# A fixed-order pipeline for the w_up stage of a diffusion block, with the w_down operands made in small steps

## The chip, the cores and the metric

The kernel runs on one core of one Trainium2 chip. The metric is the device time of one launch in microseconds, a median over several launches. One profiled execution gives the trace. The engines are named as in the profile: PE (matmuls), PEld (the weight loads of PE), DVE, ACT, POOL, and SP, which here only issues DMAs.

## The reference

One layer of a transformer-like block over 1024 tokens of width 1024, in float32. Two token mixers and their projections come first. What the change touches is the feed-forward part behind them:

```python
def swiglu(h, w_up, w_down):
    a, b = jnp.split(h @ w_up, 2, axis=-1)      # w_up: 1024 x 5632
    return (jax.nn.silu(a) * b) @ w_down        # w_down: 2816 x 1024
...
h2 = modulate(rmsnorm(x, g_ffn[l]), mod[:, 3, None], mod[:, 4, None])
x = x + mod[:, 5, None] * swiglu(h2, w_up[l], w_down[l])
return rmsnorm(x, g_final)
```

`mod` is one small matrix product of the conditioning vector, `silu(c) @ w_mod + b_mod`, in six parts of 1024.

## The kernel before, in words

**Arithmetic.** A float32 matrix product is made of three matmuls in a reduced format: each operand is split into a high part (a cast on ACT, L92) and a low part (value minus high part, on DVE, L93), and high x high, high x low and low x high add up in PSUM (`mm3`, L121 to L123). One matmul is 128x128 by 512 columns. A large product is split in 2x2 blocks and done with seven block products in place of eight (Strassen's method in Winograd's form). The operand forms are called B11, T2, T3, T1, B21, T4 and B22.

**The w_up stage** has 22 modules (`NFF`, m = 0 to 21), each 128 columns of a and 128 of b. A module loads two column blocks of w_up (`raw`, four buffers), makes four sums of them on POOL (`st`, L181, L182, L185, L195), splits seven weights (`op`, seven buffers) and runs seven products of 12 matmuls each. For m = 0 to 3 the products B11 and B21 are run earlier (`early`), so that 146 products are left. DVE adds each finished PSUM bank to the others (L184 to L200), ACT applies silu (L1017, L1020), DVE and POOL multiply (L1018, L1021), and ACT's queue stores the result to DRAM (`Gd`). The moving operands G are 28 tiles of 4 KB per partition which stay for the whole stage; the pool `slots` has 31 such places (`NS`).

**The operands of w_down.** The same stage also prepares w_down for the next one: 11 pairs of row blocks (`DPAIRS`), made between the modules m = 5 to 20 (`MADE_AT`). `down_operands` loads a pair, multiplies it by the gate row m5 on POOL (L1001, L1002), makes four differences on DVE (L1005 to L1009), splits seven forms into slots (`od`, ACT L92 and DVE L93) and stores each to DRAM by SP's queue (`Od`, L1012). The w_down stage loads them again (`form`, L1058) and casts them on ACT (L1060).

**The gate row m5** is made inside the stage: `mod_sum(5)` at m = 2 (eight 512 KB loads and eight DVE operations, L647 to L651), `mod_rows(5)` at m = 4 (L659 to L663).

**Order.** The kernel is written module by module. A planner puts the instructions of each engine's queue in an order by its own costs; each engine then runs its queue strictly in order, and an instruction that waits holds up all behind it. Only where the source says `manual_schedule` is the order of the text kept on each engine.

Of the kernel before, what the change touches and what calls it, by code (L numbers as in the profile page):

```python
# [8 lines left out]
F32 = mybir.dt.float32  # L9
F32R = mybir.dt.float32r  # L10
U8 = mybir.dt.uint8
AF = mybir.ActivationFunctionType
# [16 lines left out]
EPS = 1e-6  # L29
COL = dict(ff=0, fb=512, i=1024, q=1536, og=2048, u=2560, v=3072, ga=3584, gb=4608)  # L30
C_C, C_X, C_GM, C_GF, C_LB, C_GN, C_BM, NROW = 0, 8, 16, 24, 32, 48, 49, 97
NS = 31
RES = {1: (0, 4), 2: (1, 5), 3: (2, 6), 4: (3, 7)}
EARLY = ((), (0, 1), (2,), (3,))
H0, H1 = slice(0, HALF), slice(HALF, T)
# [3 lines left out]
def blk(i):  # L39
    return slice(i * P, (i + 1) * P)  # L40
# [3 lines left out]
def block_kernel(ctx: ExitStack, tc: tile.TileContext,  # L44
# [20 lines left out]
    def slot(name, shape=(P, T), dtype=F32):  # L65
        return slots.tile(list(shape), dtype, name=name, tag="s", bufs=NS)

    def op_slot(name):
        return slot(name, (P, 2, HALF), F32R)
# [4 lines left out]
    def ev_(name="ev"):  # L74
        return wp.tile([P, HALF], F32, name=name, tag="ev", bufs=8)

    def gl_(name="gl"):
        return wp.tile([P, HALF], F32, name=name, tag="gl", bufs=6)
# [10 lines left out]
    def split_into(o, v, hi_eng=act, lo_eng=dve):  # L89
        n = v.shape[-1]  # L90
        h, l = o[:, 0, :n], o[:, 1, :n]
        (act.copy if hi_eng is act else hi_eng.tensor_copy)(h, v)  # L92
        t_last[0] = lo_eng.tensor_tensor(l, v, h.bitcast(F32), op=ALU.subtract)  # L93
        return o
# [143 lines left out]
    def dtile(name, shape=(P, T)):  # L238
        return dram.tile(list(shape), F32, name=name)
# [3 lines left out]
    Id = [dtile(f"Id{t}", (P, HALF)) for t in range(TT)]  # L243
    Vd = [dtile(f"Vd{t}", (P, HALF)) for t in range(TT)]
    m2d = dtile("m2d")
    PBd = [dtile(f"PBd{m}") for m in range(KT)]
    X1d = [dtile(f"X1d{t}") for t in range(TT)]
    Gd = [dtile(f"Gd{m}", (P, 2, T)) for m in range(NFF // 2)]
# [393 lines left out]
    def mod_sum(j):  # L642

        a = slot("moda")
        for k in range(KT):
            raw = raw_()
            load(out=raw, in_=w_mod[blk(k), j * D:(j + 1) * D])  # L647
            if k == 0:
                dve.tensor_scalar(a, raw, sc[:, k, 0:1], None, op0=ALU.mult)
            else:  # L650
                dve.scalar_tensor_tensor(a, raw, sc[:, k, 0:1], a, op0=ALU.mult, op1=ALU.add)  # L651
        return a

    def mod_cols(j, a):
        part_sums(a, modc[:, j, :])
        dve.tensor_tensor(modc[:, j, :], modc[:, j, :], cols[:, C_BM + j * 8:C_BM + j * 8 + 8], op=ALU.add)

    def mod_rows(j, a, dst):
        load(out=dst, in_=b_mod[:, j * D:(j + 1) * D].broadcast_to([P, D]))  # L659
        for s in HS:  # L660
            ps = psx()
            pe.matmul(ps, ones, a[:, s], start=True, stop=True)
            dve.tensor_tensor(dst[:, s], ps, dst[:, s], op=ALU.add)  # L663

    rmask = const.tile([P, HALF], F32, name="rmask")
    dve.memset(rmask, 1.0)
    dve.memset(rmask.rearrange("p (c t) -> p c t", t=CH)[:, :, 0:1], 0.0)
    EA = const.tile([P, 8, 16], F32, name="EA")
# [46 lines left out]
    for n, (ka, fa, kb, fb) in enumerate(PAIRS):  # L715
        p_ = early[n] if n < len(early) else in_pair(n).head()
        if n == len(PAIRS) - 1:
            sg4 = slot("sg4", (P, 2, HALF))
            wsr, wsT = sg4[:, 0, :], sg4[:, 1, :]
            bsb = slot("bsb")[:, :HALF]  # L720
            load(out=wsr.rearrange("p (g s) -> p g s", s=P), in_=w_s[0].rearrange("g t s -> t g s"))
            load(out=bsb, in_=b_s.rearrange("a g t -> a (g t)").broadcast_to([P, HALF]))
        X, c12, c21, c22 = p_.rest(turn_ws if n == len(PAIRS) - 1 else None)
        if n == 0:
            with tc.issue_after(t_done.ins):
                for t in range(4):
                    vnorm(4 + t, vlate[t], dve)
        if ka[0] == "q":
            q = slot("q")
            act.copy(q[:, H0], X)  # L730
            pool.tensor_copy(q[:, H1], c12)
            for s, z in ((H0, c21), (H1, c22)):
                sg = gl_("sg")
                sig = after(lambda: act.activation(sg, z, AF.Sigmoid))
                pool.tensor_tensor(z, z, sg, op=ALU.mult)
                store(out=pd[kb][:, s], in_=z)
            table_use[0] = sig
            continue
        if ka[0] == "ff":
            e = ev_()  # L740
            zs = (e, c12, c21, c22)
            for z, src in zip(zs, (X, c12, c21, c22)):
                sig = after(lambda: act.activation(z, src, AF.Sigmoid))
            table_use[0] = sig
            gates(ka[1], zs, q)
        else:
            e = ev_()
            act.activation(e, X, fa)
            todo = ((ka, AF.Copy, H0, e), (ka, fa, H1, c12), (kb, fb, H0, c21), (kb, fb, H1, c22))
        for key, fn, s, z in (todo if ka[0] != "ff" else ()):  # L750
            if fn != AF.Copy:
                last_act = act.activation(z, z, fn)
            store(out=pd[key][:, s], in_=z)
        if n in (11, 13):
            ma = mod_sum({11: 3, 13: 4}[n])
        if n in (12, 14):
            mod_cols({12: 3, 14: 4}[n], ma)
        if n == 15:
            store(out=m2d, in_=mod_sum(2))
        if n == 7:  # L760
            act.activation(EA, EA, AF.Exp)
            E = EA.rearrange("p j (c i) -> p j c i", i=2)
            XA, GA, HA = (const.tile([P, 8, 8, 2], F32, name=nm) for nm in ("XA", "GA", "HA"))
            AP = const.tile([P, 8, 8], F32, name="AP")
            dve.memset(XA, 1.0)
            for dr in range(2):
                d_ = slice(4 * dr, 4 * dr + 4)
                a, b = (0, 1) if dr == 0 else (1, 0)
                Ea, Eb = E[:, d_, :, a], E[:, d_, :, b]
                X_ = XA[:, d_, :, 0]  # L770
                dve.tensor_tensor(X_, Ea, Eb, op=ALU.mult)
                dve.tensor_tensor(AP[:, d_, :], X_, X_, op=ALU.mult)
                dve.tensor_copy(GA[:, d_, :, a], Ea)
                dve.tensor_tensor(GA[:, d_, :, b], X_, Ea, op=ALU.mult)
                dve.tensor_copy(HA[:, d_, :, b], Eb)
                dve.tensor_tensor(HA[:, d_, :, a], X_, Eb, op=ALU.mult)
    dve.scalar_tensor_tensor(A2, modc[:, 4, :], 1.0, cols[:, C_GF:C_GF + 8], op0=ALU.add, op1=ALU.mult)


    V = [slot("V", (P, 2, HALF)) for _ in range(4)]  # L780
# [163 lines left out]
    def up_pair(m):  # L944
        return Strassen(lambda: load_cols(w_up, m * P, KT), lambda: load_cols(w_up, DFF + m * P, KT), G, 4)
# [41 lines left out]
                combine(F0[k][0], zs[0], F0[k][1], zs[1], k, G)  # L987

    SEG = [([0], [1])] + [([4 * i + 2, 4 * i + 3], [4 * i + 4, 4 * i + 5]) for i in range(5)]
    DPAIRS = [(ka, kb) for a, b in SEG for ka, kb in zip(a, b)]
    MADE_AT = {5 + 16 * i // 11: i for i in range(len(DPAIRS))}

    def down_operands(i):
        ka, kb = DPAIRS[i]
        ra, rb = (wp.tile([P, T], F32, name="rawd", tag="rawd", bufs=2) for _ in range(2))
        load(out=ra, in_=w_down[blk(ka), :])
        load(out=rb, in_=w_down[blk(kb), :])  # L1000
        pool.tensor_tensor(ra, ra, m5, op=ALU.mult)  # L1001
        pool.tensor_tensor(rb, rb, m5, op=ALU.mult)  # L1002
        x11, x12, x21, x22 = ra[:, H0], ra[:, H1], rb[:, H0], rb[:, H1]
        t1, t3, t4 = (gl_("t") for _ in range(3))
        dve.tensor_tensor(t1, x12, x11, op=ALU.subtract)  # L1005
        dve.tensor_tensor(t3, x22, x12, op=ALU.subtract)  # L1006
        t2 = x12
        dve.tensor_tensor(t2, x22, t1, op=ALU.subtract)
        dve.tensor_tensor(t4, x21, t2, op=ALU.subtract)  # L1009
        for nm, v in (("B11", x11), ("T1", t1), ("T3", t3), ("T2", t2), ("B22", x22), ("B21", x21), ("T4", t4)):  # L1010
            o = split_into(op_slot("od"), v)
            load(out=Od[nm, i], in_=o.bitcast(F32))  # L1012

    for m in range(NFF):
        X, c12, c21, c22 = (early[m] if m < len(early) else up_pair(m).head()).rest()
        e = ev_()
        act.activation(e, X, AF.Silu)  # L1017
        dve.tensor_tensor(e, e, c21, op=ALU.mult)  # L1018
        store(out=Gd[m // 2][:, m % 2, H0], in_=e)
        act.activation(c12, c12, AF.Silu)  # L1020
        pool.tensor_tensor(c12, c12, c22, op=ALU.mult)  # L1021
        store(out=Gd[m // 2][:, m % 2, H1], in_=c12)
        if m == 2:
            ma = mod_sum(5)
        if m == 4:
            m5 = slot("m5")
            mod_rows(5, ma, m5)
        if m in MADE_AT:
            down_operands(MADE_AT[m])


    X1 = [slot("X1") for _ in range(TT)]
# [147 lines left out]
                    for i in range(2):  # L1180
                        step(i, *st_)

    gs, O = [load_g(0, 0)], form(0)
    for s in range(len(SEG)):
        segment(s, O, gs)
        for t in RES.get(s, ()):
# [34 lines left out]
```

## Time and profile before

| what | value |
|---|---|
| median of 3 launches | 1564.56 us (1562.89 to 1566.66) |
| the profiled execution, its own time | 1563.21 us |
| its span, first to last instruction | 1561.5 us |
| PE busy | 1467.7 us, 94% of the span |
| DVE busy | 1111.4 us, 71% |
| ACT busy | 725.4 us, 46% |
| POOL busy | 610.5 us, 39% |

The span is 1.7 us shorter than the time of the same execution. PE's matmuls overlap one another: each takes some 0.39 us, and one starts every 0.23 us, so that a busy share says little and starts per microsecond say more.

### The profile page before, as it was taken

The numbers are of one execution on the slowest core, as the hardware profiler recorded it, in microseconds if no ns is written. First come the engines' busy times: TensorE is split into PE (matmuls) and PEld (weight loads), VectorE is DVE, ScalarE is ACT, GpSimd is POOL, SyncE is SP. The second block draws the span as 40 slices with busy tenths as digits, with TensorE's granted clock in tenths as the row PEclk, the third lists the DMA queues.
The fourth block names the chain that finished last, engine by engine and source line by source line (L and its number), as shares of the span: only waits on it lengthen the run. The fifth ranks groups of instructions, "written<-read, shape, count | busy, mean of one in ns | idle before, by whom it ended". The sixth has DMA issues, their size and how long they took to land. (4 is left out here: it accounts for less than half of the span.)

```text
span 1561.5 us, 19377 instructions
## 1 busy us (share of the span) xinstructions
PE 1467.7 (94%) x6754; PEld 1199.6 (77%) x6754; DVE 1111.4 (71%) x1530; ACT 725.4 (46%) x1214; POOL 610.5 (39%) x402
## 2 busy tenths in 40 slices
PE   6998999999999999999999899988878899999997
PEld 6887787777787787987788577766766788778886
DVE  2456676888767757775546987988889744577787
ACT  4355656766433332243255533334343334677645
POOL 0033143433233213344415545555464531444356
PEclk9799999999999999999999999999999999999999
DMA  9334532333677578624644163767677824599832
GB/s 308 97 121 135 149 109 68 121 122 115 209 232 228 187 256 297 225 73 133 218 148 173 58 195 115 251 237 274 240 264 257 282 82 150 187 346 357 300 115 108
DMA packets 208660, 294.41 MB, mean 189 GB/s; under 512 B 11601, under 2 KB 132018, under 8 KB 208562
## 3 DMA queue, kind: packets, MB, share of 16 engines
q1 hardware_dynamic: 183650, 245.45, 48.0%
q10 hardware_dynamic: 24912, 47.72, 8.2%
q8 instruction: 53, 0.87, 0.2%
q14 instruction: 45, 0.37, 0.1%
HBM read 202.95 MB, written 90.18 MB: 188 GB/s over the span
## 5 line engine op out<-in xcount | busy, mean ns | idle before, releaser
L93 DVE TENSOR_TENSOR op<-raw,op 128x512 fp32r<-128x512 f32 x208 | 187.4, 905 | 119.1 <-ACT op L92 118.9
L92 ACT CAST op<-raw 128x512 fp32r<-128x512 f32 x216 | 131.8, 620 | 178.4 <-PE acc L123 123.9
L121 PE MATMUL acc<-T,op 128*128 128x512 f32 x408 | 162.8, 400 | 20.9 <-DVE u L188 17.0
L121 PE MATMUL aux<-T,op 128*128 128x512 f32 x408 | 161.4, 396 | 14.2 <-DVE u L188 12.1
L122 PE MATMUL acc<-T,op 128*128 128x512 f32 x408 | 162.1, 397 | 4.8 <-DVE T L93 4.8
L93 DVE TENSOR_TENSOR op<-st,op 128x512 fp32r<-128x512 f32 x160 | 153.4, 960 | 11.8 <-ACT op L92 10.1
L123 PE MATMUL acc<-T,op 128*128 128x512 f32 x408 | 161.0, 395 | 0.0
L123 PE MATMUL aux<-T,op 128*128 128x512 f32 x408 | 160.5, 393 | 0.3 <-DVE op L93 0.3
L122 PE MATMUL aux<-T,op 128*128 128x512 f32 x408 | 160.1, 392 | 0.0
L92 ACT CAST op<-st 128x512 fp32r<-128x512 f32 x160 | 97.7, 618 | 119.3 <-PE aux L123 43.1
L181 POOL TENSOR_TENSOR st<-raw 128x512 f32<-128x512 f32 x40 | 65.4, 1635 | 193.5 <-DVE op L93 104.6
L121 PE MATMUL aux<-B,op 128*128 128x512 f32 x306 | 120.4, 393 | 8.9 <-DVE u L190 8.9
L121 PE MATMUL acc<-B,op 128*128 128x512 f32 x306 | 121.8, 398 | 7.4 <-DVE u L190 6.2
L195 POOL TENSOR_TENSOR st<-raw,st 128x512 f32<-128x512 f32 x40 | 59.9, 1498 | 155.9 <-DVE op L93 136.2
L122 PE MATMUL acc<-B,op 128*128 128x512 f32 x306 | 120.6, 394 | 0.0
L123 PE MATMUL acc<-B,op 128*128 128x512 f32 x306 | 120.6, 395 | 0.0
L123 PE MATMUL aux<-B,op 128*128 128x512 f32 x306 | 119.3, 390 | 0.4 <-DVE op L1136 0.4
L122 PE MATMUL aux<-B,op 128*128 128x512 f32 x306 | 119.3, 390 | 0.0
L121 PEld LDWEIGHTS acc<-T,op 128*128 128x128 f32 x408 | 77.8, 191 | 43.3 <-DVE u L188 21.2
L121 PEld LDWEIGHTS aux<-T,op 128*128 128x128 f32 x408 | 77.3, 189 | 35.0 <-DVE u L188 16.4
L122 PEld LDWEIGHTS acc<-T,op 128*128 128x128 f32 x408 | 78.1, 191 | 22.3 <-DVE T L93 6.7
L123 PEld LDWEIGHTS acc<-T,op 128*128 128x128 f32 x408 | 77.9, 191 | 16.3
(357 smaller groups left out, 3503.2 us busy)
## 6 DMA issues: line engine op xcount, KB each, us to landing
raw<-in_w_in_dram SPq DMA_DIRECT2D x60, 512.0 KB, 5.2
raw<-in_w_up_dram SPq DMA_DIRECT2D x46, 512.0 KB, 4.4
OdT<-od SPq DMA_DIRECT2D x44, 512.0 KB, 3.7
so<-OdT SPq DMA_DIRECT2D x44, 512.0 KB, 5.8
OdB<-od SPq DMA_DIRECT2D x33, 512.0 KB, 3.7
so<-OdB SPq DMA_DIRECT2D x33, 512.0 KB, 5.4
raw<-in_w_mod_dram SPq DMA_DIRECT2D x32, 512.0 KB, 4.1
rawd<-in_w_down_dram SPq DMA_DIRECT2D x22, 512.0 KB, 5.6
```

The source lines that it names most:

```text
L92: (act.copy if hi_eng is act else hi_eng.tensor_copy)(h, v)
L93: t_last[0] = lo_eng.tensor_tensor(l, v, h.bitcast(F32), op=ALU.subtract)
L121: pe.matmul(ps, lh, rh, start=first, stop=False, skip_group_check=cont)
L122: pe.matmul(ps, lh, rl, start=False, stop=False, skip_group_check=cont)
L123: pe.matmul(ps, ll, rh, start=False, stop=last, skip_group_check=cont)
L181: pool.tensor_tensor(s1, a21, a22, op=ALU.add)
L195: pool.tensor_tensor(s4, a12, s2, op=ALU.subtract)
```

## The change

The w_up stage is rewritten as one loop over all 146 products inside `manual_schedule`. At the step of product g, each engine's queue gets, in this order: the POOL sums of product g+5, the split of product g+4, the matmuls of g, the silu, gating and stores of earlier ones, the addition of the finished bank of g, and one or two of 13 small steps per pair of the w_down operands. These steps start at product 15 (m = 3) and are spread evenly to the end. The pair that the w_down stage uses first is made last and its seven forms stay in their slots (`made.kept`), so that it is neither stored nor loaded. Half of the multiplication by m5 moves from POOL to DVE. The gate row is made in the input projection (n = 15 and 16), kept in DRAM and loaded back; the sums for mod 3, 4 and 2 move to n = 9, 11 and 13. `NS` becomes 32; `rmask` takes a slot in place of a tile of its own.

```diff
-NS = 31
+NS = 32
-    rmask = const.tile([P, HALF], F32, name="rmask")
+    rmask = slot("rmask")[:, :HALF]
-        if n in (11, 13):
-            ma = mod_sum({11: 3, 13: 4}[n])
-        if n in (12, 14):
-            mod_cols({12: 3, 14: 4}[n], ma)
-        if n == 15:
+        if n in (9, 11, 15):
+            ma = mod_sum({9: 3, 11: 4, 15: 5}[n])
+        if n in (10, 12):
+            mod_cols({10: 3, 12: 4}[n], ma)
+        if n == 13:
             store(out=m2d, in_=mod_sum(2))
+        if n == 16:
+            m5r = slot("m5")
+            mod_rows(5, ma, m5r)
+            store(out=m5d, in_=m5r)
...
+    class DownOperands:
...
+        def hi(self, i, nm, v):
+            o = self.o[i, nm] = op_slot("od"), v
+            act.copy(o[0][:, 0, :], v)
+
+        def lo(self, i, nm):
+            o, v = self.o.pop((i, nm))
+            dve.tensor_tensor(o[:, 1, :], v, o[:, 0, :].bitcast(F32), op=ALU.subtract)
+            if i == self.pairs[-1]:
+                self.kept[nm] = [o]
+            else:
+                self.put.append((self.at, lambda: load(out=Od[nm, i], in_=o.bitcast(F32))))
+
+        def step(self, share, m5):
+            while self.at < min(self.n, share * self.n):
+                while self.put and self.put[0][0] < self.at:
+                    self.put.pop(0)[1]()
+                self.one(*self.steps[self.at], m5)
+                self.at += 1
...
+        def one(self, i, j, m5):
...
+            if j < 2:
+                for eng, z in ((dve, ra), (pool, rb)):
+                    eng.tensor_tensor(z[:, HS[j]], z[:, HS[j]], m5[:, HS[j]], op=ALU.mult)
...
+            elif j == 3:
+                t["T3"] = self.tile_("t")
+                dve.tensor_tensor(t["T3"], x22, x12, op=ALU.subtract)
+                self.hi(i, "B11", x11)
...
+            elif j == 5:
+                self.lo(i, "B11")
+                self.hi(i, "T2", x12)
...
+            elif j == 7:
+                self.lo(i, "T2")
+                if nxt is not None:
+                    self.fetch(nxt, 0)
+                self.hi(i, "B22", x22)
+            elif j == 8:
+                self.lo(i, "B22")
+                self.hi(i, "B21", x21)
+            elif j == 9:
+                self.lo(i, "B21")
+                if nxt is not None:
+                    self.fetch(nxt, 1)
+                self.hi(i, "T1", t["T1"])
+            elif j < 12:
+                nm, then = (("T1", "T3"), ("T3", "T4"))[j - 10]
+                self.lo(i, nm)
+                self.hi(i, then, t[then])
+            else:
+                self.lo(i, "T4")
...
+    LEAD = 4
+    NEW = ("B11", "T2", "T3", "T1", "B21", "T4", "B22")
+    prods = [(m, nm) for m in range(NFF) for nm in (NEW if m >= len(early) else ("T2", "T3", "T1", "T4", "B22"))]
...
+    made = DownOperands(list(range(1, len(DPAIRS))) + [0], gl_)
+    first_made = prods.index((3, "T2"))
+    with tc.manual_schedule():
+        up_loads(0)
+        up_loads(1)
+        m5 = last_gate()
+        for g in range(-LEAD - 1, N + 3):
+            if 0 <= g + LEAD + 1 < N:
+                up_sums(g + LEAD + 1)
+            if 0 <= g + LEAD < N:
+                up_split(g + LEAD)
+                m = prods[g + LEAD][0]
+                if ends[m] == g + LEAD and m + 2 < NFF:
+                    up_loads(m + 2)
+            if 0 <= g < N:
+                up_product(g)
+            for fn in todo_at.pop(g, ()):
+                fn()
+            if 0 <= g < N:
+                up_evac(g)
+            if g >= first_made:
+                made.step((g + 1 - first_made) / (N + 2 - first_made), m5)
+        made.step(1, m5)
...
-    gs, O = [load_g(0, 0)], form(0)
+    gs, O = [load_g(0, 0)], made.kept
```

## Rows read from the trace of the kernel before

**Rows 1.** The page: span and busy time of each engine

```profile
span 1561.5 us, 19377 instructions
PE 1467.7 (94%) x6754; PEld 1199.6 (77%) x6754; DVE 1111.4 (71%) x1530; ACT 725.4 (46%) x1214; POOL 610.5 (39%) x402
```

**Rows 2.** Busy us (instructions) by stretch: PE, PEld, DVE, ACT, POOL; clock, DMA share, GB/s

```profile
404.00:578.00 174.00, 170.28 (x774) 140.21 (x773) 114.34 (x144) 64.54 (x109) 42.91 (x31) 1.00 0.70 219
896.00:1250.00 354.00, 314.42 (x1305) 250.75 (x1306) 300.72 (x344) 133.67 (x235) 186.47 (x105) 0.97 0.68 233
980.00:1236.00 256.00, 220.37 (x905) 174.38 (x903) 221.71 (x252) 101.53 (x181) 136.72 (x74) 0.96 0.74 260
1250.00:1337.00 87.00, 87.00 (x386) 72.03 (x385) 37.20 (x55) 30.02 (x47) 22.67 (x19) 1.00 0.38 121
```

**Rows 3.** PE's matmuls with a T operand, 865 to 896 us: busy (instructions)

```profile
865.00:896.00 31.00, 18.32 (x62) 0.94 0.22 68
```

**Rows 4.** Who waited for whom, 896 to 1338 us: total us, times, longest us

```profile
PE acc L121 <- DVE u L188: 15.6, 5, 3.6
PE aux L121 <- DVE u L188: 10.6, 6, 3.7
PE acc L121 <- DVE u L190: 6.2, 3, 2.9
PE aux L121 <- DVE u L190: 4.7, 3, 2.2
...
ACT od L92 <- DMA OdT<-od: 68.6, 34, 3.7
ACT od L92 <- DMA OdB<-od: 39.3, 16, 4.6
...
DVE op L93 <- ACT op L92: 31.3, 19, 4.0
DVE od L93 <- ACT od L92: 26.6, 24, 3.3
```

**Rows 5.** Timeline of PE after one such wait: start us, duration us

```profile
1236.32 0.79 PE L121 MATMUL acc<-T,op 128*128 128x512 f32 x1 [3.17 <-DVE u L188]
1236.92 0.63 PE L122 MATMUL acc<-T,op 128*128 128x512 f32 x1
```

**Rows 6.** Groups of instructions, 980 to 1236 us: busy us, mean ns

```profile
L93 DVE TENSOR_TENSOR op<-st,op 128x512 fp32r<-128x512 f32 x42 | 50.5, 1202 | 0.0
...
L1001 POOL TENSOR_TENSOR rawd<-rawd,m 128x1024 f32<-128x1024 f32 x10 | 26.2, 2622 | 16.5 <-DMA rawd<-in_w_down_dram 16.5
```

**Rows 7.** Groups of instructions, 1250 to 1337 us: busy us, mean ns

```profile
L93 DVE TENSOR_TENSOR op<-st,op 128x512 fp32r<-128x512 f32 x16 | 11.1, 693 | 2.1 <-ACT op L92 1.1
...
L1021 POOL TENSOR_TENSOR m<-m,u 128x512 f32<-128x512 f32 x4 | 5.2, 1295 | 16.9 <-ACT m L1020 16.9
```

**Rows 8.** Timeline of DVE and POOL: start us, duration us

```profile
1129.18 0.68 DVE L93 TENSOR_TENSOR od<-t,od 128x512 fp32r<-128x512 f32 x1
1129.78 0.68 DVE L200 TENSOR_TENSOR m<-aux,m 128x512 f32<-128x512 f32 x1
...
1141.62 1.72 POOL L182 TENSOR_TENSOR st<-st,raw 128x512 f32<-128x512 f32 x1
1142.13 0.68 DVE L190 TENSOR_TENSOR u<-acc,u 128x512 f32<-128x512 f32 x1
...
1144.11 2.65 POOL L1002 TENSOR_TENSOR rawd<-rawd,m 128x1024 f32<-128x1024 f32 x1 [0.76 <-DMA rawd<-in_w_down_dram]
1144.42 2.89 DVE L93 TENSOR_TENSOR od<-rawd,od 128x512 fp32r<-128x512 f32 x1
```

**Rows 9.** Timeline, 889 to 894 us: the last T forms of G

```profile
890.64 0.69 DVE L93 TENSOR_TENSOR T<-z,T 128x512 fp32r<-128x512 f32 x1
891.73 1.43 POOL L93 TENSOR_TENSOR T<-t,T 128x512 fp32r<-128x512 f32 x1 [4.32 <-ACT T L92]
```

**Rows 10.** The two lines that make a gate row: ns min/median/max

```profile
L651 DVE SCALAR_TENSOR_TENSOR moda<-raw,sc,moda x28: 1271/1284/1892, 419.6 to 916.0; 128x1024 f32<-128x1024 f32 x28
L662 PE MATMUL aux<-moda,ones x4: 592/593/593, 959.8 to 961.1; 128*128 128x512 f32 x4
```

**Rows 11.** DMA issues, 896 to 1337 us: count, KB, median us to landing

```profile
OdT<-od SPq DMA_DIRECT2D x44, 512.0 KB, 3.7
```

**Rows 12.** Casts of reloaded w_down operands, 1250 to 1337 us: busy us, mean ns

```profile
L1060 ACT CAST T<-so 128x1024 fp32r<-128x1024 f32 x4 | 4.2, 1050 | 1.7 <-DMA so<-OdT 1.7
L1060 ACT CAST B<-so 128x1024 fp32r<-128x1024 f32 x3 | 3.0, 1042 | 1.0 <-DMA so<-OdB 1.0
```

More of the change, by code (lines that the diff above doesn't have):

```diff
@@ L245, in block_kernel @@
     m2d = dtile("m2d")
+    m5d = dtile("m5d")
     PBd = [dtile(f"PBd{m}") for m in range(KT)]
@@ L777, in block_kernel, with last_gate, __init__, fetch @@
     dve.scalar_tensor_tensor(A2, modc[:, 4, :], 1.0, cols[:, C_GF:C_GF + 8], op0=ALU.add, op1=ALU.mult)
+    SEG = [([0], [1])] + [([4 * i + 2, 4 * i + 3], [4 * i + 4, 4 * i + 5]) for i in range(5)]
+    DPAIRS = [(ka, kb) for a, b in SEG for ka, kb in zip(a, b)]
+    def last_gate():
+        z = slot("m5")
+        load(out=z, in_=m5d)
+        return z
+    class DownOperands:
+        def __init__(self, pairs, tile_):
+            self.pairs, self.tile_ = list(pairs), tile_
+            self.raw, self.t, self.o, self.put, self.kept = {}, {}, {}, [], {}
+            self.steps = [(i, j) for i in self.pairs for j in range(13)]
+            self.n, self.at = len(self.steps), 0
+            self.fetch(self.pairs[0], 0)
+            self.fetch(self.pairs[0], 1)
+        def fetch(self, i, j):
+            z = self.raw[i, j] = wp.tile([P, T], F32, name="rawd", tag="rawd", bufs=2)
+            load(out=z, in_=w_down[blk(DPAIRS[i][j]), :])
+        def hi(self, i, nm, v):
[14 more added lines that the diff above has]
+                self.at += 1
+            if share >= 1:
+                while self.put:
+                    self.put.pop(0)[1]()
+        def one(self, i, j, m5):
+            ra, rb = self.raw[i, 0], self.raw[i, 1]
+            x11, x12, x21, x22 = ra[:, H0], ra[:, H1], rb[:, H0], rb[:, H1]
+            t = self.t
+            nxt = self.pairs.index(i) + 1
+            nxt = self.pairs[nxt] if nxt < len(self.pairs) else None
+            if j < 2:
+                for eng, z in ((dve, ra), (pool, rb)):
+                    eng.tensor_tensor(z[:, HS[j]], z[:, HS[j]], m5[:, HS[j]], op=ALU.mult)
+            elif j == 2:
+                t["T1"] = self.tile_("t")
+                dve.tensor_tensor(t["T1"], x12, x11, op=ALU.subtract)
+            elif j == 3:
+                t["T3"] = self.tile_("t")
+                dve.tensor_tensor(t["T3"], x22, x12, op=ALU.subtract)
+                self.hi(i, "B11", x11)
+            elif j == 4:
+                dve.tensor_tensor(x12, x22, t["T1"], op=ALU.subtract)
+            elif j == 5:
+                self.lo(i, "B11")
+                self.hi(i, "T2", x12)
+            elif j == 6:
+                t["T4"] = self.tile_("t")
+                dve.tensor_tensor(t["T4"], x21, x12, op=ALU.subtract)
+            elif j == 7:
[17 more added lines that the diff above has]
+                self.lo(i, "T4")
@@ L987, in block_kernel @@
                 combine(F0[k][0], zs[0], F0[k][1], zs[1], k, G)
[L992 to L1029, printed above, removed]
+    LEAD = 4
@@ new lines, in block_kernel, with up_loads @@
+    NEW = ("B11", "T2", "T3", "T1", "B21", "T4", "B22")
+    prods = [(m, nm) for m in range(NFF) for nm in (NEW if m >= len(early) else ("T2", "T3", "T1", "T4", "B22"))]
+    ends = {m: max(g for g, (m_, _) in enumerate(prods) if m_ == m) for m in range(NFF)}
+    UP = [None] * NFF
+    todo_at = {}
+    class UpState:
+        pass
+    def up_loads(m):
+        u = UP[m] = UpState()
+        u.p = early[m] if m < len(early) else None
+        if u.p is not None and u.p.ra is not None:
+            u.ra = u.p.ra
+        else:
+            u.ra = load_cols(w_up, m * P, KT)
+        u.rb = load_cols(w_up, DFF + m * P, KT)
+        u.o = {}
+        u.a = dict(B11=u.ra[:, H0], B21=u.ra[:, H1], T4=u.rb[:, H1])
@@ new lines, in up_sums, with st @@
+    def up_sums(g):
+        m, nm = prods[g]
+        u = UP[m]
+        a11, a12, a21, a22 = u.ra[:, H0], u.ra[:, H1], u.rb[:, H0], u.rb[:, H1]
+        def st():
+            return wp.tile([P, HALF], F32, name="st", tag="st", bufs=4)
+        if nm == "T2":
+            s1, s2 = st(), st()
+            pool.tensor_tensor(s1, a21, a22, op=ALU.add)
+            pool.tensor_tensor(s2, s1, a11, op=ALU.subtract)
+            u.a["T1"], u.a["T2"] = s1, s2
+        elif nm == "T3":
+            s3 = u.a["T3"] = st()
+            pool.tensor_tensor(s3, a11, a21, op=ALU.subtract)
+        elif nm == "B22":
+            s4 = u.a["B22"] = st()
+            pool.tensor_tensor(s4, a12, u.a["T2"], op=ALU.subtract)
@@ new lines, in up_split, with up_product @@
+    def up_split(g):
+        m, nm = prods[g]
+        UP[m].o[nm] = wop(UP[m].a[nm])
+    def up_product(g):
+        m, nm = prods[g]
+        u = UP[m]
+        if nm in ("B11", "T2") and not hasattr(u, "bank"):
+            p = u.p if u.p is not None else up_pair(m)
+            u.bank = dict(zip("YZW", (f() for f in p.banks[1:])))
+            u.bank["X"] = u.p.X if u.p is not None else p.banks[0]()
+            u.m1 = u.p.m1 if u.p is not None else ev_("m1")
+        ps = u.bank[dict(B11="X", T2="Y", T3="W", T1="Z", B21="X", T4="W", B22="Z")[nm]]
+        first = nm in ("B11", "T2", "T3", "T1")
+        for k in range(4):
+            mm3(ps, hl(u.o[nm], blk(k)), hl(G[nm][k]), first and k == 0, k == 3, not first)
@@ new lines, in later, with up_evac, gate @@
+    def later(g, fn):
+        todo_at.setdefault(g, []).append(fn)
+    def up_evac(g):
+        m, nm = prods[g]
+        u = UP[m]
+        b = u.bank
+        if nm == "B11":
+            act.copy(u.m1, b["X"])
+        elif nm == "T2":
+            dve.tensor_tensor(u.m1, b["Y"], u.m1, op=ALU.add)
+            if u.p is not None:
+                u.e = ev_()
+                act.activation(u.e, b["X"], AF.Silu)
+        elif nm == "T3":
+            u.u3 = ev_("u3")
+            dve.tensor_tensor(u.u3, b["W"], u.m1, op=ALU.add)
+        elif nm == "T1":
+            dve.tensor_tensor(u.u3, b["Z"], u.u3, op=ALU.add)
+        elif nm == "B21":
+            u.e = ev_()
+            act.activation(u.e, b["X"], AF.Silu)
+        elif nm == "T4":
+            c21 = ev_("c21")
+            dve.tensor_tensor(c21, b["W"], u.m1, op=ALU.add)
+            dve.tensor_tensor(u.e, u.e, c21, op=ALU.mult)
+            later(g + 1, lambda: store(out=Gd[m // 2][:, m % 2, H0], in_=u.e))
+        else:
+            dve.tensor_tensor(u.m1, b["Z"], u.m1, op=ALU.add)
+            def gate():
+                act.activation(u.m1, u.m1, AF.Silu)
+                pool.tensor_tensor(u.m1, u.m1, u.u3, op=ALU.mult)
+            later(g + 1, gate)
+            later(g + 2, lambda: store(out=Gd[m // 2][:, m % 2, H1], in_=u.m1))
```

1 line of the change is left out of this document (added).

## The prediction

> **What bounds the kernel now.** I began with the page [rows 1]: PE is busy 94% of the span, so PE sets the time, and the question is where it starts matmuls more slowly than it can. The windows view answers that. From 1250 to 1337 us, the last part of the w_up stage, 386 matmuls are seen in 87 us [rows 2], one every 0.2265 us; no pair of w_down is being made there. A product of 12 matmuls so costs 2.72 us at PE's pace. From 896 to 1250 us the same stage shows 1305 matmuls in 354 us [rows 2]. Some five are of another kind or straddle the edges, so 1300 x 0.2265 = 294.5 us would do, and **59.5 us** are lost. Nothing else in the profile is so large: the input projection has 774 matmuls in 174 us [rows 2], at the same pace.
>
> Why, the view of waits tells [rows 4]. PE waits for DVE's bank additions (four rows, 37.1 us, up to 3.7 us at once), DVE for ACT's casts (57.9 us), and ACT for the store of an earlier w_down form (107.9 us in 50 waits). The G tiles hold 28 of 31 slots and m5 one, so two are left for seven forms per pair, and ACT, which runs in order, stands at the next form's cast until a store has landed (3.7 us, [rows 11]). After a wait PE is slow as well: behind 3.17 us idle it starts matmuls 0.43 to 0.6 us apart instead of 0.2265 [rows 5]. The granted clock is 0.97 over the stretch, that is some 6% of it at 1.2 instead of 2.4 GHz, about 10 us of the 59.5.
>
> A second limit lies under the first. DVE starts an operation of 512 columns every 0.60 us [rows 8], and its split of a sum took 0.69 us in the quiet part [rows 7], but 1.20 us between 980 and 1236 us [rows 6]. In the timeline a split that reads two SBUF tiles takes 2.89 us and ends 0.55 us after the POOL multiplication beside it, while an addition that reads PSUM keeps its 0.68 us under a POOL operation [rows 8]. So POOL time and two-input DVE time mostly add up.
>
> **Part 1: fixed order and even spreading.** If the casts no longer hold up the splits, the 140.8 products left at 896 us run at PE's pace: minus 59.5 us. For that each engine must keep up with a product every 2.72 us. Made operands now spread over 133 products for 11 pairs, 12.09 products or 32.8 us of PE to a pair. In that cycle DVE has 12.1 splits, 8.6 additions from PSUM, 1.7 multiplications and the pair's own 13 operations (two multiplications, four differences, seven splits): 35.4 x 0.60 = 21.2 us. POOL has 6.9 sums, 1.7 gatings and two half multiplications: 10.6 x 1.29 [rows 7] = 13.7 us. How far the two add up I take from 980 to 1236 us: 252 DVE operations are 151 us; POOL's 54 short ones at 1.29 and 20 long ones at 2.6 [rows 2, 6] are 122 us; that is 273 in 256, so 86% of POOL's time stood in DVE's way. Then the cycle needs 21.2 + 0.86 x 13.7 = 33.0 us against PE's 32.8: even. Bounds: nothing, if DVE's additions and idle time cover more of POOL; (21.2 + 13.7 - 32.8) x 11 = **22 us**, if nothing overlaps. I take **+5 us**, near the packing seen, since a fixed order can swap less.
>
> The Trainium skill, SBUF — State Buffer, § Who interferes with whom, says that a DVE instruction with two SBUF inputs and a GpSimd instruction that reads SBUF shut each other out for their whole length, and one with a single SBUF input is not touched; rows 8 agree (2.89 against 0.68 us). By that rule alone only 26.8 DVE operations count, 16.1 + 13.7 = 29.8 us per cycle, so the port by itself would cost nothing; the sum by the rows would take 33.0.
>
> ACT has per cycle 19.1 casts and some 5.2 copies and silus of 0.6 us, 14.6 of 32.8 us. Three slots are now free for forms (32 less 28 less one). A step lasts 32.8 / 13 = 2.5 us; the cast of step 9 needs the slot of the form split at step 7 and stored at step 8, which lands about 3.7 us later, 1.3 us after step 9 begins. The same holds for steps 10 and 11. Behind the waiting cast on ACT stands the next weight's cast, four products (10.9 us) ahead of PE. That lead is the cover, so I cost it at nothing; without it, 33 x 1.3 = 43 us.
>
> **Part 2: the start of the stage.** The planner ran T products of several modules side by side while the last T forms came in: 62 T matmuls, 5.2 products, by 896 us [rows 3]. In a fixed order T2 of module 0 must end before T3 begins. Its last form is ready at 891.3 us, T3's at 893.2 [rows 9]; then T2 ends at 892, T3 at 894.7, and half of T1 is done by 896: 2.5 products. Loss 2.7 x 2.72 = **+7 us** (0, if DVE and POOL come to these forms sooner without mod_sum and the other module's work; 12 with a slow clock behind the wait).
>
> **Part 3: the gate row.** Eight DVE operations of 1.28 us and four half-speed matmuls [rows 10] leave the stage and enter the input projection, with eight loads of 512 KB. DVE is busy there for 114 of 174 us, the DMAs at 0.70 [rows 2]; the idle 60 us of DVE hide the 10.3. What is not hidden is PE's queue at the sums of the row: four matmuls 1.9 us, which come out of the 59.5 as well. I take **+2 us**; if DVE there were the bound, 11 us more than now; nothing, if hidden.
>
> **Part 4: the hand-over to w_down.** Seven stores, seven loads and seven casts (7.2 us, [rows 12]) go away, but lie beside PE's full pace today, so they give nothing. In return the first G tiles must be split behind the last gates in the same queues: one add, silu, cast and split, 0.68 + 0.63 + 0.6 + 0.7 us, against a similar wait now. **+2 us**; from 2 us gained, if the lighter ACT helps, to 8 lost, if the kept pair's last form is late.
>
> **Sum.** -59.5 + 5 + 7 + 2 + 2 = -43.5 us. The profiled execution took 1563.2 us (span 1561.5): 1519.7. The median of the runs shown is 1.4 us above it: **1521 us**.
>
> **Rivals.**
> - *The port becomes the bound.* With no overlap, 22 us in place of 5: 1538 us. For it: 86% is already close to all, and the fixed order interleaves POOL sums with every DVE chain. Against it: PSUM additions are a quarter of DVE's operations and run free.
> - *The slot wait stays.* If stores land later than 3.7 us and ACT's standstill eats the lead, 43 us come back: 1564, no change. For it: ACT's 107.9 us of waits are the largest row now. Against it: three slots instead of two and 32.8 us for a pair, where now ten pairs pass in 256.
> - *Slower: everything in line.* DVE's queue now holds split, addition (which waits for PE), and step in one row. If POOL's 1.13 us per product, DVE's own 1.76 and its waits for ACT (57.9 us over 141 products, 0.41) all stand one behind the other, a product costs 3.30 us: 133 x 0.58 = 77 us, so -59.5 + 77 + 11 = +29, 1593 us. It decides from 3.08 us per product on. Against it: a lead of four products makes only the sum of busy time count, not each wait.
>
> **How the numbers follow.** Forecast 0.64, port 0.20, slot wait 0.07, in line 0.09. A measurement tells this kernel from no change at about 0.2%, 3 us. The range reaches from near all lower ends of the costs together (1563.2 - 59.5 - 2 + 1.4 = 1503) to a little over the port's case: 1505 to 1546; the last two cases stay outside. The forecast's own range is 1507 to 1534. Faster: the first two cases and half of the third, 0.88; same 0.03; slower 0.09.
>
> **What would show it.** In the profile after: a stage at one matmul per 0.2265 us and clock 1.00 but for its first 10 us; no PE wait for bank additions above 1 us; ACT's waits for Od stores some 30 of about 1 us; DVE busy near nine tenths. Wrong, if DVE is full while PE has gaps all along (port), if PE's gaps follow ACT's Od waits (slots), or if the input projection grows by more than 5 us.

## The result and the profile after

The changed kernel takes **1545.01 us** (median of 4 launches, 1543.4 to 1547.31) against 1563.79 us before: ratio 0.9878, 95% interval 0.9859 to 0.9897, that is 18.8 us faster. Forecast were 1521 us and 42 to 44 us of gain. The sign held and the time lies just inside the range; the gain is less than half of what was forecast.

The profiled execution took 1543.4 us. First two lines of the page of the changed kernel, which answer to [rows 1]:

```profile
span 1541.7 us, 19297 instructions
PE 1461.0 (95%) x6754; PEld 1196.2 (78%) x6754; DVE 1127.9 (73%) x1552; ACT 715.5 (46%) x1207; POOL 600.9 (39%) x402
```

To see where the time went, the stages are cut at the same events. The first line below is of the kernel before, the second of the changed one: matmuls that read tile T (the forms T1 to T4 of G), from the start of the w_up stage on (the first of the two times is the start of the first).

```profile
L121 PE MATMUL acc<-T,op x160: 389/389/794, 865.4 to 1277.8; 128*128 128x512 f32 x160
```

```profile
L121 PE MATMUL acc<-T,op x176: 388/390/796, 879.2 to 1294.3; 128*128 128x512 f32 x176
```

And the last silu of the stage, before (L1020) and after (L1176); the second time is the start of the last one:

```profile
L1020 ACT ACTIVATE m<-m x22: 622/632/635, 911.5 to 1339.3; 128x512 f32<-128x512 f32 x22
```

```profile
L1176 ACT ACTIVATE m<-m x22: 626/632/634, 915.2 to 1319.3; 128x512 f32<-128x512 f32 x22
```

The stage starts 13.8 us later and ends 20.0 us earlier; from there to the end it is 222.2 us before and 222.4 after. So 33.8 us were gained inside the stage and 13.8 us lost ahead of it. The windows view of the changed kernel gives T matmuls alone in the first 31 us of the stage, which answers to [rows 3] (62 there), and all engines for the input projection and the steady part, which answer to [rows 2]:

```profile
879.00:910.00 31.00, 14.03 (x42) 0.78 0.25 68
```

```profile
404.00:592.00 188.00, 175.44 (x771) 140.64 (x769) 123.00 (x156) 65.91 (x112) 49.29 (x34) 0.98 0.70 221
950.00:1319.00 369.00, 356.71 (x1541) 290.50 (x1542) 319.40 (x377) 142.89 (x256) 180.63 (x112) 0.99 0.62 210
```

The same 770 or so matmuls of the input projection take 188 us instead of 174. In the steady part 1541 matmuls x 0.2265 = 349 us would do, and 369 are taken: 20 us are still lost. The waits of the changed kernel there, which answer to [rows 4]:

```profile
PE aux L121 <- DVE u L1161: 7.7, 5, 2.2
PE acc L121 <- DVE u L1161: 2.8, 2, 2.2
...
ACT od L813 <- DMA OdT<-od: 49.5, 10, 9.9
ACT od L813 <- DMA OdB<-od: 42.2, 17, 6.2
...
DVE op L93 <- ACT op L92: 36.7, 17, 5.3
DVE od L817 <- ACT od L813: 6.9, 2, 3.4
```

PE waits for DVE's additions for 12.0 us (four rows, two of them shown) instead of 37.1. But ACT still stands 91.7 us at forms whose slot has not come free (107.9 before), 27 times, once for 9.9 us. The timeline shows what such a standstill does:

```profile
973.49 0.62 ACT L813 CAST od<-t 128x512 fp32r<-128x512 f32 x1 [9.86 <-DMA OdT<-od]
974.01 0.62 ACT L92 CAST op<-st 128x512 fp32r<-128x512 f32 x1
974.53 0.59 ACT L1166 ACTIVATE ev<-acc 128x512 f32<-128x512 f32 x1
974.66 0.69 DVE L93 TENSOR_TENSOR op<-st,op 128x512 fp32r<-128x512 f32 x1 [5.28 <-ACT op L92]
```

ACT waits for a store, the next weight's cast stands behind it, and DVE, whose next split needs that cast, stands still for 5.28 us with bank additions queued behind.

The form that waits here is T1, cast at step 9 of its pair; it needs the slot of T2. T2's split ended at 964.18 us, but its store went out behind three loads on SP's queue, and the cast started 7.7 us after the store's issue:

```profile
964.24 0.34 SPq L809 DMA_DIRECT2D rawd<-in_w_down_dram  x1
964.75 1.00 SPq L103 DMA_DIRECT2D raw<-in_w_up_dram  x2
965.81 1.96 SPq L821 DMA_DIRECT2D OdT<-od  x1
```

It is so in every pair that is stored: the ten waits of the row `OdT` are all this cast, 3.1 to 9.9 us long (4.9 on average). In the source T2's store always stands behind the load of the next pair's first block (step 7), and the cast started 5.1 to 7.7 us (5.6 on average) after that store's issue.

### The profile page after: what moved, and what is told of

It is laid out like the page before. It is cut to its first block, busy times and chain, and to the rows that moved or that the text cites. A ratio compares the mean times of both kernels' runs of the same rounds, so it can differ in the third digit from the quotient of the medians.

```text
span 1541.7 us, 19297 instructions
## 1 busy us (share of the span) xinstructions
PE 1461.0 (95%) x6754; PEld 1196.2 (78%) x6754; DVE 1127.9 (73%) x1552; ACT 715.5 (46%) x1207; POOL 600.9 (39%) x402
## 4 chain that ended last, share of the span: by engine, by line
PE 46%; DVE 15%; issue 13%; DMA 11%; POOL 8%; ACT 6%; SPq 1%; ACTq 0%; POOLq 0%; DVEq 0%
PE acc L121 8%; PE acc L123 8%; PE acc L122 8%; DVE op L93 4%; PE aux L121 4%; PE aux L122 4%; PE aux L123 4%; DMA raw<-in_w_mod_dram 4%; PE aux L316 2%; DMA raw<-in_w_in_dram 1%; POOL rawd L841 1%; DMA OdB<-od 1%; ACT op L92 1%; DMA OdT<-od 1%; POOL st L1126 1%
## 5 line engine op out<-in xcount | busy, mean ns | idle before, releaser
L93 DVE TENSOR_TENSOR op<-raw,op 128x512 fp32r<-128x512 f32 x208 | 195.6, 945 | 100.6 <-ACT op L92 98.3
L93 DVE TENSOR_TENSOR op<-st,op 128x512 fp32r<-128x512 f32 x160 | 144.4, 904 | 40.2 <-ACT op L92 39.3
L121 PE MATMUL acc<-T,op 128*128 128x512 f32 x400 | 159.9, 400 | 13.6 <-ACT T L92 6.1
L121 PE MATMUL aux<-T,op 128*128 128x512 f32 x400 | 158.5, 396 | 12.2 <-DVE u L1161 7.7
L122 PE MATMUL acc<-T,op 128*128 128x512 f32 x400 | 159.2, 398 | 4.0 <-DVE T L93 4.0
L123 PE MATMUL acc<-T,op 128*128 128x512 f32 x400 | 157.9, 395 | 0.0
L122 PE MATMUL aux<-T,op 128*128 128x512 f32 x400 | 157.1, 393 | 0.0
L123 PE MATMUL aux<-T,op 128*128 128x512 f32 x400 | 156.2, 392 | 0.0
L121 PE MATMUL aux<-B,op 128*128 128x512 f32 x300 | 118.1, 394 | 5.9 <-DVE u L190 4.7
L121 PE MATMUL acc<-B,op 128*128 128x512 f32 x300 | 117.6, 393 | 3.0 <-ACT m L165 1.8
L123 PE MATMUL acc<-B,op 128*128 128x512 f32 x300 | 117.5, 392 | 1.6 <-DVE op L93 1.6
L122 PE MATMUL aux<-B,op 128*128 128x512 f32 x300 | 117.0, 390 | 0.0
L122 PE MATMUL acc<-B,op 128*128 128x512 f32 x300 | 116.9, 390 | 0.0
L123 PE MATMUL aux<-B,op 128*128 128x512 f32 x300 | 116.9, 390 | 0.0
L1177 POOL TENSOR_TENSOR m<-m,u 128x512 f32<-128x512 f32 x22 | 34.3, 1559 | 180.4 <-ACT m L1176 180.4
L121 PEld LDWEIGHTS acc<-T,op 128*128 128x128 f32 x400 | 76.5, 191 | 34.8 <-ACT T L92 8.0
L181 POOL TENSOR_TENSOR st<-raw 128x512 f32<-128x512 f32 x18 | 32.6, 1812 | 170.3 <-DMA raw<-in_w_in_dram 127.3
L122 PEld LDWEIGHTS acc<-T,op 128*128 128x128 f32 x400 | 76.5, 191 | 21.3 <-DVE T L93 5.5
L123 PEld LDWEIGHTS acc<-T,op 128*128 128x128 f32 x400 | 76.3, 191 | 16.0 <-issue 0.2
```

Of the source, the lines that this page charges most:

```text
L121: pe.matmul(ps, lh, rh, start=first, stop=False, skip_group_check=cont)
L122: pe.matmul(ps, lh, rl, start=False, stop=False, skip_group_check=cont)
L123: pe.matmul(ps, ll, rh, start=False, stop=last, skip_group_check=cont)
L181: pool.tensor_tensor(s1, a21, a22, op=ALU.add)
L1177: pool.tensor_tensor(u.m1, u.m1, u.u3, op=ALU.mult)
```

## The experiments

Ratios are to the kernel before, run beside each version on the same chip; the changed kernel's is 0.9878. "The steady part" is the stretch of some 1540 matmuls from about 70 us behind the stage's start to its end (369 us in the changed kernel, 349 at PE's pace).

**mod_late: the gate row made in the w_pa loop.**

```diff
-        if n in (9, 11, 15):
-            ma = mod_sum({9: 3, 11: 4, 15: 5}[n])
...
+        if n in (11, 13):
+            ma = mod_sum({11: 3, 13: 4}[n])
...
+        if m == 4:
+            m5a = mod_sum(5)
+        if m == 6:
+            m5r = slot("m5")
+            mod_rows(5, m5a, m5r)
+            store(out=m5d, in_=m5r)
```

> The changed kernel, with the gate row made in the w_pa loop (its sums at m = 4, its row at m = 6) in place of the input projection; the sums for mod 3, 4 and 2 go back to n = 11, 13 and 15. If the 14 us by which the w_up stage now starts later come from the eight extra loads and sums (raw buffers and SP's queue shared with the w_in columns), it takes 10 to 14 us less than the changed kernel: 1531 to 1535. If they come from a planner's order that differs for other reasons (32 slots, rmask in a slot), less than 3 us: 1542 to 1545. If the w_pa stage can't hide the sums either, 1541 to 1547 with the loss now between 720 and 870 us.

1549.7 us, ratio 0.9901 (0.9881 to 0.9922): not told apart from the changed kernel. The input projection is as before again (the next stage starts at 699 us, 698 before, 712 changed), though the 32 slots and `rmask` in a slot stayed: these two are not what costs there. But PE now waits once for 19.6 us in the w_pa loop:

```profile
PE acc L121 <- ACT op L92: 19.6, 1, 19.6
```

The third case of the expectation: the loss moved. The weights of w_pa come through the same raw buffers and SP's queue as the eight loads.

**even: the casts spread over the steps.** The same instructions; only the steps at which forms are cast and split change (L813, L817), with B21 now second of the seven and one load a step earlier.

```diff
+                if j == 1:
+                    self.hi(i, "B11", x11)
...
             elif j == 3:
...
-                self.hi(i, "B11", x11)
+                self.hi(i, "B21", x21)
```

> The changed kernel with the casts of the seven w_down forms spread over the 13 steps (at 1, 3, 5, 7, 9, 10, 11 in place of 3, 5, 7, 8, 9, 10, 11); the same instructions, nothing added or removed. If ACT's standstill at a slot whose store has not landed (91.7 us in all) starts PE's losses in the steady part, ACT's waits for Od stores fall below 30 us, PE's waits for the bank additions nearly vanish, and the kernel takes 8 to 18 us less: 1527 to 1537. If the port that DVE and POOL share is the bound, the waits of ACT fall but the stage keeps its length within 3 us: 1542 to 1546.

1542.48 us, ratio 0.9852 (0.9827 to 0.9876); the interval overlaps the changed kernel's.

```profile
952.00:1315.00 363.00, 354.40 (x1543) 291.07 (x1542) 316.83 (x378) 143.51 (x255) 182.59 (x113) 0.99 0.63 213
ACT od L813 <- DMA OdB<-od: 30.3, 9, 8.6
ACT od L813 <- DMA OdT<-od: 16.5, 6, 5.1
```

ACT's waits for Od stores fall from 91.7 to 46.8 us, the steady part takes 363 us: 6 us of 20 are won, in one profile. That is too small an effect for the first case; the time meets the second (1542 to 1546), the stage doesn't.

**one_store: no store, no wait.** The stores of pairs 2 to 10 are left out, and the w_down stage loads the first stored pair's forms for every pair.

```diff
-            else:
+            elif i == self.pairs[0]:
                 self.put.append(...)
...
-                load(out=..., in_=Od[nm, DPAIRS.index(pair)])
+                load(out=..., in_=Od[nm, 1])
```

> The changed kernel, with only the first pair's forms stored; the w_down stage loads that pair's forms for every pair, so that pairs 2 to 10 are computed with the wrong weights. Slots of the other pairs come free with their split, so that no cast waits for a store. Slots as the cause: ACT's Od waits vanish and the kernel takes 10 to 20 us less, 1525 to 1535; if even gains as much as this, the store itself costs nothing else. Port as the bound: 1541 to 1546.

1528.76 us, ratio 0.9771 (0.9745 to 0.9797). The windows row of its steady part:

```profile
949.00:1302.00 353.00, 350.39 (x1543) 288.95 (x1542) 318.14 (x378) 143.50 (x256) 184.06 (x113) 1.00 0.40 125
```

DVE's 378 operations and POOL's 113 are all still there, with the same busy times (318 and 184 us; 319 and 181 in the changed kernel), in 16 us less, at 4 us above PE's pace. So the shared port alone doesn't bound the stage. The expectation's first case (slots as the cause) is met. But fewer stores are also less traffic (DMA share 0.40 instead of 0.62), so this run alone doesn't tell the slots from the traffic.

**no_mult: less for DVE and POOL, all stores kept.** The multiplication of w_down by the gate row is left out.

```diff
             if j < 2:
-                for eng, z in ((dve, ra), (pool, rb)):
-                    eng.tensor_tensor(z[:, HS[j]], z[:, HS[j]], m5[:, HS[j]], op=ALU.mult)
+                pass
```

> The changed kernel without the multiplication of w_down by the gate row (left out: 22 half multiplications on DVE, 22 on POOL). Some 13 us of DVE and 28 us of POOL leave the stage; the stores and slots stay. Port as the bound: PE's losses in the steady part vanish, 15 to 20 us less than the changed kernel, 1525 to 1530. Slots alone: at most 4 us less, 1541 to 1545. Between the two, 1530 to 1540, if the standstill only costs because a full DVE can't catch up again.

1527.77 us, ratio 0.9763 (0.9743 to 0.9784): its steady part is PE's pace, with no wait of PE at all.

```profile
953.00:1302.00 349.00, 349.00 (x1541) 288.97 (x1541) 281.29 (x355) 141.47 (x253) 144.96 (x90) 1.00 0.66 221
```

```profile
ACT od L813 <- DMA OdT<-od: 16.1, 8, 3.3
...
ACT od L813 <- DMA OdB<-od: 9.0, 5, 5.2
```

The time is that of the port's case (1525 to 1530). Taken alone it would say that DVE and POOL are the bound, as one_store alone says that the stores are: either cure takes nearly all of the loss, so neither limit costs the 20 us by itself. Traffic as such isn't the cause either, since the DMA share is 0.66 here. With less for DVE and POOL to do, ACT's waits for slots shrink from 91.7 to 25.1 us though no slot was added. The run takes 22 operations from DVE and 22 from POOL, so it doesn't tell the shared port from DVE's own time.

**even_now: even, and each store queued behind its split at once.** The edit against even:

```diff
                 self.one(*self.steps[self.at], m5)
                 self.at += 1
+                while self.put:
+                    self.put.pop(0)[1]()
```

> even, and each store is queued on SP directly behind the split of its form and not one step later. If the slots' time to come free is what counts, this takes most of what one_store took: the stage from 952 us on runs in 353 to 358 us in place of 363, the kernel 5 to 10 us less than even. If a store behind DVE's late splits is late anyway, less than 3 us.

1533.32 us, ratio 0.9794 (0.9774 to 0.9814): 9 us less than even and clear of the changed kernel. The first case is met: the steady part takes 357 us for 1543 matmuls, with the work of the changed kernel whole.

```profile
951.00:1308.00 357.00, 351.26 (x1543) 288.77 (x1542) 315.92 (x379) 143.08 (x255) 180.26 (x112) 1.00 0.65 216
ACT od L813 <- DMA OdB<-od: 34.0, 10, 6.2
ACT od L813 <- DMA OdT<-od: 14.6, 8, 4.7
```

Only the stores' places in SP's queue differ from even, so the earlier stores are what gained. ACT's waits for them didn't get less in sum (48.6 us against 46.8), only the longest did (6.2 against 8.6): the sum of these waits doesn't say what PE loses, and by which wait the 6 us come was not taken apart.

**planned: the loop without a fixed order.**

```diff
-    with tc.manual_schedule():
+    with nullcontext():
```

> The changed kernel with the same loop, but without manual_schedule: the planner orders the engines' queues. If the fixed order is what gains, this is slower than the changed kernel by 10 us or more. If the gain is in the even spreading of the 13 steps and in the two places more for forms, it is within 5 us of the changed kernel, and its first 30 us of the stage come out like those of the kernel before.

1569.06 us, ratio 1.0020 (1.0002 to 1.0038): all of the gain is gone. From the stage's first T matmul (880.1 us) to its last silu (1343.4) it takes 463.3 us, the changed kernel 440.1 and the kernel before 473.9. So of the 33.8 us inside the stage, some 11 are there without the order (the even spreading, the added slots and the moved row), and the order adds 23; the later start of the stage eats the 11. The casts of weights on ACT wait for PE again, 62 us in these two rows (60.5 in the kernel before between 950 and 1339 us, 3.3 in the changed one from 902 us on). In the source such a cast can wait for PE only through its buffer, one of seven, which an earlier product still reads; how the planner's order brings that about was not taken apart:

```profile
ACT op L92 <- PE acc L123: 35.5, 17, 3.7
ACT op L92 <- PE aux L123: 26.8, 14, 2.1
```

**late_slots and late_spread: the row in w_pa, through slots.** In late_slots all eight loads come at m = 0, in late_spread two at each of m = 0 to 3. In place of mod_late's lines for m = 4 they have, first late_slots, then late_spread (the row follows at m = 5):

```diff
+        if m == 0:
+            m5a = mod_sum(5, lambda: slot("mraw"))
...
+        if m < 4:
+            m5a = mod_sum(5, lambda: slot("mraw"), m)
```

> The gate row made in the w_pa loop as in mod_late, but its eight loads go into eight free slots at m = 0 and not into the four raw buffers that also bring the weights of w_pa. If mod_late lost its 22 us between 699 and 774 us because weights queued for those buffers, the loss there falls below 4 us and the w_up stage starts within 4 us of the kernel before (865 us), so that the kernel takes 10 to 14 us less than the changed one. If the eight sums on DVE or the 4 MB are what costs, 15 us or more stay and it takes no less than the changed kernel.

> late_slots with the eight loads spread, two at each of m = 0 to 3 of the w_pa loop. If the 11.7 us wait of late_slots comes from the other loads queued on SP behind a burst of 4 MB, it falls below 4 us, the w_up stage starts at 864 to 869 us, and the kernel takes 11 to 15 us less than the changed one: 1530 to 1534. If the eight sums on DVE are what the w_pa stage can't take, a wait of 8 us or more stays and it is no faster than late_slots.

1540.49 us, ratio 0.9839 (0.9818 to 0.9860), and 1541.66 us, ratio 0.9859 (0.9837 to 0.9882). The w_up stage starts at 874.4 and 870.9 us (879.2 changed, 865.4 before). In late_slots PE waits once for some 11 us in w_pa (first row below), in late_spread 6.0 us in two waits of the same kind, for DVE's work on the gate tiles, and 2.0 us at the row itself:

```profile
PE acc L121 <- DVE g L900: 12.2, 2, 11.3
PE acc L121 <- DVE g L902: 6.0, 2, 3.6
PE aux L665 <- DVE moda L654: 2.0, 1, 2.0
```

Both gained less than expected, and by their intervals neither is told apart from the changed kernel: no place tried takes the row for nothing. That spreading the loads shortens the wait fits loads queued on SP behind the burst, as the expectation had it; the eight sums on DVE stay as a cause of the rest.

**row_one_load and row_none: what in the input projection costs.** The first leaves out seven of the row's eight loads, the second the row's loads, sums and matmuls, and takes the bias alone:

```diff
-            raw = raw_()
-            load(out=raw, in_=w_mod[blk(k), j * D:(j + 1) * D])
+            if j != 5 or k == 0:
+                raw = raw_()
+                load(out=raw, in_=w_mod[blk(k), j * D:(j + 1) * D])
...
-        if n in (9, 11, 15):
-            ma = mod_sum({9: 3, 11: 4, 15: 5}[n])
+        if n in (9, 11):
+            ma = mod_sum({9: 3, 11: 4}[n])
...
-            mod_rows(5, ma, m5r)
+            load(out=m5r, in_=b_mod[:, 5 * D:6 * D].broadcast_to([P, D]))
```

> The changed kernel, but the sums of the gate row in the input projection all read the first of the eight loaded tiles, so that seven loads (3.5 MB, seven turns of a raw buffer) are left out and the row is wrong. All eight DVE sums stay. If the loads in the buffers of the w_in columns cost the 14 us, the w_up stage starts at 865 to 869 us and the kernel takes 10 us less than the changed one. If the sums on DVE cost, it starts within 3 us of the changed kernel's 879.

> The changed kernel without the sums of the gate row (only its bias is loaded, stored and used, so that the row is wrong); the sums for mod 3, 4 and 2 stay at n = 9, 11 and 13. If the gate row itself costs the 14 us, the w_up stage starts at 864 to 868 us. If the earlier places of the other three sums, where DVE still works on the gates of the heads, cost, it still starts at 874 us or later.

1539.18 us, ratio 0.9863 (0.9815 to 0.9912), and 1536.5 us, ratio 0.9851 (0.9809 to 0.9893). By their intervals neither time is told apart from the changed kernel's. The stage starts at 876.2 and 873.8 us. Even without the row it starts 8.4 us later than before, so most of the 13.8 us is the earlier place of the other sums. The rest can't be divided: in the six profiles whose code ahead of the stage is the same as the changed kernel's (changed, even, one_store, no_mult, even_now, planned) it starts between 878.6 and 882.3 us, so steps of 2 or 3 us are within what repeats differ by. First in the kernel before, then in the changed one, the first sum of mod 3 (first of the times):

```profile
L649 DVE TENSOR_SCALAR moda<-raw,sc x4: 749/753/755, 414.6 to 891.3; 128x1024 f32<-128x1024 f32 x4
```

```profile
L650 DVE TENSOR_SCALAR moda<-raw,sc x4: 753/753/754, 374.1 to 509.2; 128x1024 f32<-128x1024 f32 x4
```

In row_none the timeline shows the harm: DVE still works at the gates of the last head (L705), the column block of w_in waits for a raw buffer behind the row blocks of w_mod, ACT waits 4.49 us for it, and POOL, which has stood idle for 29.15 us, begins its next sums only at 412.12 us (in the kernel before POOL's longest idle time between 396 and 440 us is 6.06 us):

```profile
405.01 0.68 DVE L705 TENSOR_TENSOR u<-B,u 128x512 f32<-128x512 f32 x1
405.62 1.28 DVE L652 SCALAR_TENSOR_TENSOR moda<-raw,sc,moda 128x1024 f32<-128x1024 f32 x1
...
408.29 0.62 ACT L92 CAST op<-raw 128x512 fp32r<-128x512 f32 x1 [4.49 <-DMA raw<-in_w_in_dram]
...
412.12 1.26 POOL L181 TENSOR_TENSOR st<-raw 128x512 f32<-128x512 f32 x1 [29.15 <-DVE u L188]
```

**best and best2: the pieces together.** even_now with the gate row of late_slots (best) or late_spread (best2), and at the stage's start the products T2, T3 and T1 of module 0 run with their first three row blocks before the fourth, which comes late:

```diff
+            if g == 0:
+                for h in range(3):
+                    up_product(h, range(3))
+                up_product(0, (3,))
...
```

> late_slots and even_now together, and at the start of the stage the matmuls with the first three row blocks of T2, T3 and T1 of module 0 before those with the fourth, which comes late. If the causes are apart from one another, their gains add up: 12 + 10 + 4 us less than the changed kernel, 1514 to 1523. If the stage's DVE backlog eats one with the other, 1524 to 1532.

> best with the eight loads spread as in late_spread. 8 to 12 us less than best: 1514 to 1519. If the planner's order in the w_pa stage costs again elsewhere, 1520 to 1527.

1526.63 us, ratio 0.9759 (0.9736 to 0.9782), and **1525.44 us, ratio 0.9752 (0.9729 to 0.9775)**, the fastest version of this study, some 20 us under the changed kernel. Both meet only the second case of their expectations, and best2 is not told apart from best. What the new order of the stage's first products gives was not run by itself.

## Why the prediction was wrong

From the profiled executions, each part by the events above; the four add up to the span's -19.8 us:

| part | forecast | measured |
|---|---|---|
| up to the stage's start (Part 3) | +2 | +13.8 |
| first 31 us of the stage (Part 2) | +7 | 20 fewer matmuls x 0.2265 = +4.5 |
| steady part (Part 1) | -59.5 + 5 = -54.5 | 60.1 lost before, 21.8 after: -38.3 |
| behind the stage (Part 4) | +2 | +0.2 |

- **Why PE was slow before: right in the main.** With no_mult's smaller work PE takes the steady part without a gap. With the work whole no version got all of the 59.5 us: best2, the fastest, has 1533 matmuls in 356 us there and still loses some 9.
- **Part 1, the cost of the slot wait: the step that failed.** It was put at 1.3 us three times a pair, covered by the lead of four products, "so I cost it at nothing". Measured are 91.7 us of standstill in 27 waits. The cast of step 9 stood 4.9 us on average, not 1.3: it started 5.6 us after the issue of the store that it needs, not 3.7 (in every pair that store goes out behind a load); and ACT was at the cast 0.7 us after that issue, not a step of 2.5 us later. And the lead covers PE only while DVE can make up for lost time. The prediction's own sum had DVE and POOL at 33.0 of 32.8 us: a lane that full has nothing to make up with. I priced each limit alone and cleared it alone; one_store (353 us) and no_mult (349 us) show that the 20 us come from the two together. That a full DVE can't win the lead back is the reading that fits both runs; no run measures it directly.
- **Part 1, the port: right.** +2 by the sum, 4 us above PE's pace in one_store, where the port's work is whole and the waits for stores are gone. By the Trainium skill's rule (SBUF — State Buffer, § Who interferes with whom), as the prediction worked it out, the port by itself would cost nothing; 4 us fit that as well as the sum's 2. The rival with 22 us has the right size by accident: its mechanism, no overlap at all, is not what happened. The rival of the slot wait had the right mechanism and too high a price (43 us). (Two small slips: by its own terms the bound without overlap is 23 us, and 3.7 less 2.5 leaves 1.2 us, so 40 and not 43. Neither changes the outcome.)
- **Part 3: wrong, and for a part left out.** Only the gate row was costed. The change also moves the sums for mod 3, 4 and 2 two loop turns ahead, into a stretch where DVE still makes the heads' gates and w_in's blocks need the same four buffers. row_none puts that at some 8 us of the 13.8; the rest is the row, and how much of it is sums and how much loads is not shown (2.4 and 3.0 us by one profile each, less than repeats differ by). "The idle 60 us of DVE hide the 10.3" took a mean over 174 us for a cover that its first turns didn't have.
- **Part 2: mechanism right,** size 4.5 instead of 7.
- **The signs.** Two of the signs of being wrong that the prediction named have come: the input projection grew by 14 us, and ACT's waits for Od stores are not some 30 of about 1 us, but 27 of up to 9.9. That 1545 us lies inside the range confirms nothing of the sum: it took a loss of 16 us in Part 1 and of 12 in Part 3 to get there.
- **The order itself**, which the prediction took for granted, is what carries the change: without it (planned) nothing is gained in the whole time.

Left open: no run shows how much of mod_late's 19.6 us is the raw buffers and how much SP's queue, and the start of the stage, where PE waits for the last T forms, was not taken apart.

## What to carry to other kernels

Two limits that each just fit need not be free together: where an engine is planned as full as here (33.0 of 32.8 us), a wait that "a lead covers" can turn into loss, because little time is left to win the lead back. When an order is written by hand, count how long a buffer stays taken, from its first write to the landing of its store and the store's place in its queue, before counting busy time. And cost every line that the diff moves, even two loop turns, at the place where it lands, by that stretch's own rows and not by a stage's mean.

## What the runs showed of the hardware

After a wait PE did not always fall to half speed at once. Behind 2.18 us of idle time in the changed kernel it started a matmul at 991.49 us and five more at about the usual distance, at a granted clock of 0.97 (991.0 to 992.9 us). Only then the distance went to 0.43 us for some 3 us, at a granted clock of 0.50 (993.2 to 995.8 us, the lower of the two levels, 1.2 GHz), though it had work all the time:

```profile
991.80 0.40 PE L122 MATMUL aux<-T,op 128*128 128x512 f32 x1
992.04 0.39 PE L123 MATMUL aux<-T,op 128*128 128x512 f32 x1
...
993.09 0.63 PE L121 MATMUL aux<-T,op 128*128 128x512 f32 x1
993.52 0.63 PE L122 MATMUL aux<-T,op 128*128 128x512 f32 x1
```

So the slowdown behind a wait can stand away from the wait in the trace. In [rows 5], behind 3.17 us, it was there from the first matmul on (granted clock 0.50 from 1236.3 to 1238 us).
